# Order of products, bank copies and step size in an mLSTM + sliding-window layer on one core

## The chip, the cores and the metric

The kernel runs on one core of one Trainium2 chip. The metric is the device time of one execution in microseconds, the median of several runs. A profiled execution leaves a trace of every instruction on the five engines: PE (TensorE, matrix products, with its weight loads listed as PEld), DVE (VectorE), ACT (ScalarE), POOL (GpSimd) and SP (SyncE, which here issues most DMA transfers).

## The reference

One layer of an encoder is computed for a prompt of 2048 rows and for 8 sequences of 16 sample rows (together 17 tiles of 128 rows, width 1024). One projection makes all inputs of two groups of heads: four mLSTM heads of 128 (a matrix memory, in chunks) and eight query heads over two key heads of 64 with rotation of positions, a window of whole chunks, and a learned sink per head. Both are concatenated, projected, added to the input and normalised. A ConvFFN follows (up-projection, causal convolution of width 3, a gate, down-projection, normalisation). Cut to what matters here:

```python
def trunk_layer(x, pos, C0, n0, m0, k_cache, v_cache, conv_prev, mchunk, ...):
    qm, km, vm, om, ip, fp, qa, ka, va = split_in(x @ w_in)
    km = km.reshape(B, T, M_HEADS, M_HEAD_DIM) * (M_HEAD_DIM ** -0.5)
    logi = ip + b_igate
    logf = jax.nn.log_sigmoid(fp + b_fgate)
    hm, C1, n1, m1 = mlstm_chunkwise(qm, km, vm, logi, logf, C0, n0, m0, mchunk)
    og = jax.nn.sigmoid(om)
    hm = (og * head_norm(hm, g_mlstm_norm)).reshape(B, T, M_WIDTH)
    qa = rope(qa.reshape(B, T, A_Q_HEADS, A_HEAD_DIM), pos)
    ka = rope(ka.reshape(B, T, A_KV_HEADS, A_HEAD_DIM), pos)
    ha = swa_prompt(qa, ka, va, attn_sinks)      # swa_step with the cache for the sample rows
    mix = jnp.concatenate([hm, ha], axis=-1) @ w_out
    h = layer_norm(DEEPNORM_ALPHA * x + mix, ln1_g, ln1_b)
    f, conv_rows = conv_ffn(h, conv_prev, w_up, w_conv, b_conv, w_down)
    y = layer_norm(DEEPNORM_ALPHA * h + f, ln2_g, ln2_b)
```

The outputs are both `y`, the mLSTM states, the last keys and values, and the last rows of the convolution's input. All is float32.

## The kernel before

**Products.** Every large product is split into a high and a low part of its operands (`split`: an ACT copy to the rounded type, then a DVE subtraction), and takes three matmuls per block of 128 rows of the contraction. The in-projection, the up- and the down-projection also use a Strassen-like scheme: a product of 2 x 2 blocks is made from seven block products, numbered 1 to 7, and sums of operands and of results.

**In-projection** (`i_begin`, `i_dense`, `i_product`, `i_after`). The tokens come in four blocks of four tiles (`IBLOCKS`, the first with the sample tile 16 added), the weights in five groups: group 0 and 1 are q and k of the mLSTM heads, 2 the queries of the attention, 3 the output gate, 4 the values v. For each block and group the seven products run on three PSUM banks, A (products 1 and 2), B (6, 5 and 3) and C (7 and 4), in the order that `i_begin` writes into `self.items`. `i_after` takes the results out: after 6 the bank B is copied to `u2`, after 2 bank A goes out, after 5 bank B is copied to `u4`, C is added and it goes out, after 4 C is added to `u2` and it goes out, after 3 bank B goes out and A (which holds product 1 of the next group) is copied to B. `i_out` sends a result on: group 2 through `rope` (the rotation; it reads the bank on DVE and adds on POOL), group 3 through a tanh, the others through an ACT copy, and then `i_store` writes it to DRAM (zqk, zqa, zog, zv). `i_direct` makes gates, keys and values of a tile without the scheme, on banks A and C (L707); `i_keys` takes them out, rotates the keys and stores zkv.

**Mixing** runs as three chains of Python generators, `m_chain` (mLSTM), `a_chain` (attention) and `t_sample` (the sample rows), in PE's order between the dense products. `Chains` keeps a planner's clock: each dense piece adds its cost, and a chain's next step is written into the order once its due time has come. A step yields its own cost on PE and the delay to the next step; `until` forces steps where the out-projection needs a tile. PE's order is exactly this written order; the other engines' orders are made by a scheduler from priorities. PE takes its instructions strictly in order, so a mixing product whose input is late holds back the dense products behind it. All chains share five PSUM banks (`bank`). Per tile the mLSTM chain makes running sums (`m_rows`, product pgr), scores, transposed keys and row weights (pscore, pkt, pm, pcol), results and state update (pnum, pcu: `m_tile`), the norm (`m_norm`) and transposes (pht, `m_out`); the attention chain transposes queries and keys (pq, pk), makes scores (psc), transposes them (ppt) and multiplies by values (ppo).

**Out-projection and passage.** `o_block` multiplies five blocks of tiles (`OBLOCKS`) with w_out, adds alpha times x, normalises (`norm_steps`) and writes zh. `x_pair` loads and splits the mixed inputs. While the last block runs, `f_hT` loads tiles of zh (`hst`, issued from ACT's queue) and transposes them for the up-projection (fht, L1593). `f_setup` opens the pool of the ConvFFN and loads its constants. `f_ups`, `f_product`, `f_after` and `f_downs` are the ConvFFN, the larger half of the time.

## Time and profile before

| | us |
|---|---|
| median of 3 runs | 2481.56 |
| lowest and highest run | 2476.81 and 2483.23 |
| the profiled execution's own time | 2475.97 |
| its span, first to last instruction | 2473.9 |
| PE busy in the span | 2358.5 |

The stages by time in the trace: the in-projection with mixing between its products lasts from 0 to 742 us, the out-projection with the rest of mixing to about 1005, the passage into the ConvFFN to about 1020, and the ConvFFN to the end. In rows of busy time, "x" counts instructions; a wait row names the engine and line that waited, what ended the wait, the total in us, the number of times and the longest. The granted clock of PE is a share of full speed.

### The profile page before, as it was taken

The page shows a single profiled execution, that of the slowest core. Times are in us where ns is not written, and L with a number is a line of the kernel's source. Part 1 is how long each engine was busy: PE and PEld are TensorE (multiplying, and loading weights), DVE is VectorE, ACT ScalarE, POOL GpSimd, SP SyncE. Part 2 cuts the span into 40 slices and gives each one's busy share as a digit, 9 for nine tenths or more (in the row PEclk, how much of TensorE's full clock was granted, in tenths as well). Part 3 has the DMA queues.
Part 4 walks back from the last instruction along what each step waited for, and adds up shares of the span by engine and source line. Part 5 has one row for each costly group of instructions (what it writes and reads, how often), then busy time and mean ns, then how long its engine had stood idle before and what let it go on. Part 6 is the DMA issues. An engine that isn't in the chain of part 4 may idle for free.

```text
span 2473.9 us, 39844 instructions
## 1 busy us (share of the span) xinstructions
PE 2358.5 (95%) x14425; PEld 2160.9 (87%) x14425; DVE 1838.3 (74%) x3211; ACT 1240.5 (50%) x2250; POOL 361.8 (15%) x369
## 2 busy tenths in 40 slices
PE   8999989998999889799999999999999999999998
PEld 8989888998987767699999999999999978778776
DVE  8677477678656767698788876778766677796897
ACT  5343265565554443555555555555544544444553
POOL 0101111311222333210000000002000000220400
PEclk9999899999999999899999999999999999999999
DMA  8889877878777445578777789987998876656663
GB/s 292 312 290 320 287 220 242 278 237 282 254 254 241 157 162 183 211 274 298 276 281 264 276 302 321 307 301 234 315 304 262 262 266 213 227 181 210 218 188 106
DMA packets 296932, 625.23 MB, mean 253 GB/s; under 512 B 46876, under 2 KB 140064, under 8 KB 296736
## 3 DMA queue, kind: packets, MB, share of 16 engines
q1 hardware_dynamic: 294144, 613.25, 73.5%
q0 software_dynamic: 1728, 6.29, 0.7%
q10 hardware_dynamic: 864, 3.15, 0.3%
q8 instruction: 114, 1.87, 0.3%
q14 instruction: 82, 0.67, 0.1%
HBM read 452.04 MB, written 170.56 MB: 252 GB/s over the span
## 4 chain that ended last, share of the span: by engine, by line
PE 64%; DVE 10%; DMA 6%; issue 3%; ACT 3%; POOL 2%; SPq 0%; DVEq 0%; ACTq 0%; POOLq 0%
PE dps L1728 17%; PE fup L1728 17%; PE dps L681 7%; PE fht L1931 5%; PE dps L1931 5%; PE fup L1931 3%; PE dps L212 1%; PE dps L213 1%; PE dps L214 1%; DVE w L208 1%; PE ppo L1272 1%; DVE uw L208 1%; ACT sc L1253 1%; PE ppt L1266 1%; DMA txy<-wdn 1%
## 5 line engine op out<-in xcount | busy, mean ns | idle before, releaser
L1728 PE MATMUL dps<-hh,uw 128*128 128x384 f32 (+1 forms) x1848 | 481.1, 329 | 6.8 <-ACT u L1753 1.9
L1728 PE MATMUL fup<-hh,uw 128*128 128x384 f32 (+1 forms) x1848 | 480.2, 328 | 3.0 <-ACT u L1753 2.5
L1728 PEld LDWEIGHTS dps<-hh,uw 128*128 128x128 f32 x1848 | 330.0, 188 | 9.9 <-ACT u L1753 2.5
L1728 PEld LDWEIGHTS fup<-hh,uw 128*128 128x128 f32 x1848 | 330.1, 188 | 4.3 <-ACT u L1753 3.3
L1776 DVE SCALAR_TENSOR_TENSOR cc<-u,cw,cc 128x768 f32<-128x768 f32 (+1 forms) x264 | 252.4, 977 | 107.8 <-ACT cc L1774 105.8
L1728 PE MATMUL fup<-hl,uw 128*128 128x384 f32 (+1 forms) x924 | 302.8, 328 | 2.6 <-DVE hl L208 2.6
L1728 PE MATMUL dps<-hl,uw 128*128 128x384 f32 (+1 forms) x924 | 302.5, 327 | 0.0
L681 PE MATMUL dps<-w,oh 128*128 128x256 f32 x1344 | 263.0, 290 | 12.0 <-ACT zev L757 6.7
L208 DVE TENSOR_TENSOR w<-wraw,w 128x1024 fp32r<-128x1024 f32 (+2 forms) x167 | 206.2, 1244 | 61.4 <-ACT w L207 54.6
L207 ACT CAST w<-wraw 128x1024 fp32r<-128x1024 f32 (+2 forms) x167 | 162.9, 984 | 156.4 <-PE dps L681 74.1
L681 PEld LDWEIGHTS dps<-w,oh 128*128 128x128 f32 x1344 | 217.0, 193 | 24.9 <-issue 8.1
L207 ACT CAST uw<-wraw 128x1024 fp32r<-128x1024 f32 x126 | 122.9, 977 | 202.4 <-PE dps L1931 95.3
L208 DVE TENSOR_TENSOR uw<-wraw,uw 128x1024 fp32r<-128x1024 f32 x126 | 150.7, 1197 | 61.6 <-ACT uw L207 61.4
L681 PE MATMUL dps<-w,ol 128*128 128x256 f32 x672 | 191.2, 285 | 0.0
L1774 ACT ACTIVATE cc<-u,cw 128x768 f32<-128x768 f32 (+1 forms) x132 | 129.6, 998 | 119.6 <-DVE u L1767 60.6
L681 PE MATMUL dps<-oh,w 128*128 128x256 f32 x896 | 176.4, 291 | 13.8 <-DVE zev L761 5.7
L1931 PE MATMUL fup<-uw,fu 128*128 128x512 f32 x726 | 176.4, 399 | 8.9 <-DVE yacc L1960 4.5
L1728 PEld LDWEIGHTS fup<-hl,uw 128*128 128x128 f32 x924 | 173.5, 188 | 3.2 <-DVE hl L208 3.2
L1931 PEld LDWEIGHTS fup<-uw,fu 128*128 128x128 f32 x726 | 137.0, 189 | 44.0 <-DVE yacc L1960 5.4
L1728 PEld LDWEIGHTS dps<-hl,uw 128*128 128x128 f32 x924 | 173.6, 188 | 0.0
L681 PEld LDWEIGHTS dps<-oh,w 128*128 128x128 f32 x896 | 145.4, 194 | 24.2 <-DVE zev L761 6.9
L1931 PE MATMUL dps<-uw,fu 128*128 128x512 f32 x660 | 164.7, 395 | 0.0
(346 smaller groups left out, 4777.0 us busy)
## 6 DMA issues: line engine op xcount, KB each, us to landing
uw<-zw SPq DMA_DIRECT2D x176, 512.0 KB, 5.1
zw<-uw SPq DMA_DIRECT2D x88, 512.0 KB, 2.9
w<-zws SPq DMA_DIRECT2D x72, 512.0 KB, 5.5
wv<-wup SPq DMA_DIRECT2D x66, 512.0 KB, 5.5
wraw<-wi SPq DMA_DIRECT2D x65, 512.0 KB, 5.3
wraw<-zt SPq DMA_DIRECT2D x60, 512.0 KB, 3.9
wraw<-wdn SPq DMA_DIRECT2D x45, 512.0 KB, 3.8
wraw<-wo SPq DMA_DIRECT2D x40, 512.0 KB, 4.2
```

The costliest lines, as they stand in the source:

```text
L207: nc.scalar.copy(hi, src)
L208: nc.vector.tensor_sub(lo, src, hi.bitcast(F32))
L212: mm(out, ah, bh, start=start, stop=False)
L213: mm(out, ah, bl, start=False, stop=False)
L214: mm(out, al, bh, start=False, stop=stop)
L681: mm(o, l, r, start=s in (1, 7) and c == k == i == 0, stop=k == 3 and i == 2, skip_group_check=True)
L1253: nc.scalar.activation(sc[:, j, :N], sc[:, j, :N], AF.Exp, bias=mx[:, j:j + 1], scale=0.125, accum_out=sm[:, j:j + 1])
L1266: nc.tensor.transpose(pp[:, j * P:(j + 1) * P], scs[kvh][:, j, kt * P:(kt + 1) * P], self.ident)
L1728: mm(ps, l[:, k], r[:, k], start=s in (1, 7) and k == 0 and i == 0, stop=k == 3 and i == 2, skip_group_check=True)
L1774: S.activation(c[:, v], u[:, v, 2:2 + n], AF.Identity, bias=w[3], scale=w[2])
L1776: V.scalar_tensor_tensor(c[:, v], u[:, v, i:i + n], w[i], c[:, v], op0=ALU.mult, op1=ALU.add)
L1931: mm(ps, l[:, k, c], r[:, k], start=s in (1, 4, 7) and u == 0 and k == 0 and i == 0, stop=u == nu - 1 and k == n - 1 and i == 2, skip_grou ...
```

## The change

The diff leaves the arithmetic of the layer as it is, and the numbers of instructions on PE, DVE, POOL and SP too; ACT gets 60 more.

1. In-projection, blocks 1 to 3: within a group the products run 6, 7, 2, 5, (1 of the next group), 3, 4 in place of 6, 2, 5, (1), 4, 3, (7 of the next group); in the last group 6, 7, 5, 2, 3, 4 in place of 6, 2, 5, 3, 4. Block 0 keeps its order. The steps that prepare the next block's tokens are attached to other products.
2. Results leave their banks by ACT copies; `rope` works in place on the copy in SBUF. `u2` is a buffer of the ring `zev`, which has six buffers in place of four. The pair angles have two buffers in place of three.
3. The norm's scale g is no longer multiplied into the gate on DVE: `m_out` applies it in the copy out of the bank (four ACT instructions of 128 columns in place of one of 512).
4. Mixing: steps are cut finer (`m_tile`, `m_masked`, `m_exps`, `m_scaled`, `swa_first`, `swa`), with other delays; loads (`m_load`, `swa_dma`, `swa_cache`) are issued one step or more ahead; the denominators' exponential reads an SBUF copy.
5. The sample rows' convolution buffers `sconv` and `convs` move from the pool opened in `f_setup` to one opened in `f_ups`, and the load of `sconv` with them.

```diff
-                if g:
-                    it += [("p", b, g, s) for s in (6, 2)]
-                it.append(("p", b, g, 5))
-                if g + 1 < NG:
-                    it += [("p", b, g + 1, 1)] * (b + g > 0) + [("p", b, g, 4), ("p", b, g, 3), ("p", b, g + 1, 7)]
+                if b == 0:
+                    it += [("p", b, g, s) for s in (6, 2)] * (g > 0) + [("p", b, g, 5)]
+                    if g + 1 < NG:
+                        it += [("p", b, g + 1, 1)] * (g > 0) + [("p", b, g, 4), ("p", b, g, 3), ("p", b, g + 1, 7)]
+                    else:
+                        it += [("p", b, g, 3), ("p", b, g, 4)]
+                elif g + 1 < NG:
+                    it += [("p", b, g, s) for s in (6, 7, 2)] * (g > 0)
+                    it += [("p", b, g, 5), ("p", b, g + 1, 1), ("p", b, g, 3), ("p", b, g, 4)]
                 else:
-                    it += [("p", b, g, 3), ("p", b, g, 4)]
+                    it += [("p", b, g, s) for s in (6, 7, 5, 2, 3, 4)]
...
     def i_keys(self, b, ti, ps):
...
+        kv = self.mp.tile([P, 2 * P], F32, name="kve", tag="kve", bufs=2)
+        nc.scalar.copy(kv, ps[:, 8:264])
         nc.scalar.copy(self.gates[b][:, ti, :], ps[:, :8])
-        kv = self.mp.tile([P, 2 * P], F32, name="kve", tag="kve", bufs=2)
-        nc.scalar.copy(kv[:, P:], ps[:, 136:264])
-        self.rope(ps[:, 8:136], kv[:, :P], t, 1, nc.vector)
+        self.rope(kv[:, :P], t, 1, nc.vector, self.zev())
...
-    def i_gate(self, ev, i):
-        v = ev.rearrange("p (c m) -> p c m", c=2)
-        gm = self.gm[:, i * HT:(i + 1) * HT].rearrange("p (o m) -> p o m", o=1).to_broadcast([P, 2, HT])
-        self.nc.vector.scalar_tensor_tensor(v, v, 1.0, gm, op0=ALU.add, op1=ALU.mult)
...
-        if g == 2:
-            A = self.zev()
-            self.rope(src, A, IBLOCKS[b][2 * j], 2, nc.gpsimd)
-            self.i_store(b, g, i, j, A)
-            return
...
-            self.i_gate(ev, i)
+            nc.vector.tensor_scalar_add(ev, ev, 1.0)
...
+        if g == 2:
+            self.rope(ev, IBLOCKS[b][2 * j], 2, nc.gpsimd)
...
-            self.u2 = self.mp.tile([P, 512], F32, name="u2", tag="u2", bufs=1)
+            self.u2 = self.zev()
...
-    def rope(self, src, A, t, nt, adder):
+    def rope(self, A, t, nt, adder, B=None):
...
-        n = src.shape[-1]
-        B = self.mp.tile([P, 512], F32, name="rb", tag="rb", bufs=1)[:, :n]
+        n = A.shape[-1]
+        if B is None:
+            B = self.mp.tile([P, 512], F32, name="rb", tag="rb", bufs=1)
+        B = B[:, :n]
...
-        w = lambda z: z.rearrange("p (t x d) -> p t x d", t=nt, d=32)
-        V.tensor_mul(w(A), w(src), cos.to_broadcast([P, nt, n // (32 * nt), 32]))
+        w = A.rearrange("p (t x d) -> p t x d", t=nt, d=32)
...
-        V.tensor_mul(h(B, 0), h(src, 1), over(ms))
-        V.tensor_mul(h(B, 1), h(src, 0), over(sin))
+        V.tensor_mul(h(B, 0), h(A, 1), over(ms))
+        V.tensor_mul(h(B, 1), h(A, 0), over(sin))
+        V.tensor_mul(w, w, cos.to_broadcast([P, nt, n // (32 * nt), 32]))
...
-        r = self.mp.tile([P, nt, 3, 32], F32, name="ropet", tag=f"ropet{nt}", bufs=2 * nt - 1)
+        r = self.mp.tile([P, nt, 3, 32], F32, name="ropet", tag=f"ropet{nt}", bufs=nt)
...
-        return self.mp.tile([P, 512], F32, name="zev", tag="zev", bufs=4)
-    def gm_load(self):
-        nc = self.nc
-        self.gm = self.mp.tile([P, 512], F32, name="gm", tag="gm", bufs=1)
-        nc.sync.dma_start(self.gm, self.a["gm"].to_broadcast([P, 512]))
-        nc.vector.tensor_scalar_mul(self.gm, self.gm, 0.5)
+        return self.mp.tile([P, 512], F32, name="zev", tag="zev", bufs=6)
...
-        col = self.work("col", [P, 8], bufs=2)
-        nc.vector.tensor_copy(col[:, c0:8], ps[:, c0:8])
+        col = self.work("col", [P, 40], bufs=2)
+        nc.vector.tensor_copy(col[:, c0:], ps[:, c0:])
+        return col
+    def m_emt(self, col):
         emt = self.work("emt", [P, MH], bufs=2)
-        nc.scalar.activation(emt, ps[:, 36:40], AF.Exp)
-        return col, emt
+        self.nc.scalar.activation(emt, col[:, 36:40], AF.Exp)
+        return emt
...
-                pend = self.m_rows(t, b, ti)
+                pend = self.m_load(t, b, ti), *self.m_rows(t, b, ti)
...
-            hn = self.m_norm(*(yield from self.m_tile(t, b, ti, *pend)))
+            hn = self.m_norm(*(yield from self.m_tile(t, *pend)))
             pend = None
+            yield 950, 3000
+            self.m_scaled(hn)
             if t + 1 < NPT and self.i_done > self.place(t + 1)[0]:
-                pend = self.m_rows(t + 1, *self.place(t + 1))
+                pend = self.m_load(t + 1, *self.place(t + 1)), *self.m_rows(t + 1, *self.place(t + 1))
             yield 300, 9000
-            self.m_out(t, hn)
+            self.m_out(t, hn[0])
...
-    def m_weights(self, pm, col, mask):
-        nc = self.nc
+    def m_masked(self, pm, mask):
         dt = self.work("dt", [P, MH, P])
-        nc.vector.tensor_tensor(dt, pm, mask.rearrange("p (o m) -> p o m", o=1).to_broadcast([P, MH, P]), op=ALU.add)
+        self.nc.vector.tensor_tensor(dt, pm, mask.rearrange("p (o m) -> p o m", o=1).to_broadcast([P, MH, P]), op=ALU.add)
+        return dt
+    def m_exps(self, dt, col):
         for h in range(MH):
-            nc.scalar.activation(dt[:, h], dt[:, h], AF.Exp, bias=col[:, 4 + h:5 + h])
-        return dt
+            self.nc.scalar.activation(dt[:, h], dt[:, h], AF.Exp, bias=col[:, 4 + h:5 + h])
...
-        V.tensor_mul(s, s, r)
+        return hn, s, r
+    def m_scaled(self, hn):
+        hn, s, r = hn
+        self.nc.vector.tensor_mul(s, s, r)
         for h in range(MH):
-            nc.scalar.activation(hn[:, h], hn[:, h], AF.Copy, scale=s[:, h:h + 1])
-        return hn
+            self.nc.scalar.activation(hn[:, h], hn[:, h], AF.Copy, scale=s[:, h:h + 1])
...
-        nc.scalar.copy(mix, ps)
+        for h in range(MH):
+            nc.scalar.activation(mix[:, h], ps[:, h], AF.Copy, scale=self.gm[:, h:h + 1])
...
-    def m_tile(self, t, b, ti, i, mp):
+    def m_tile(self, t, load, i, mp):
...
-        qk, v1, og = self.m_load(t, b, ti)
+        qk, v1, og = load
+        pm = self.m_rep(i)
+        col = self.m_cols(i, mp)
+        dt = self.m_masked(pm, self.mcau)
+        yield 600, 3000
+        emt = self.m_emt(col)
...
-        pm = self.m_rep(i)
-        col, emt = self.m_cols(i, mp)
         wi = self.m_inter(pm, col)
-        dt = self.m_weights(pm, col, self.mcau)
+        self.m_exps(dt, col)
+        nc.gpsimd.tensor_mul(qk[:, 0:4], qk[:, 0:4], wi)
+        yield 950, 6000
         sd = self.m_weighted(ps, dt)
-        nc.gpsimd.tensor_mul(qk[:, 0:4], qk[:, 0:4], wi)
...
-        yield 1900, 7500 if ti == 0 else 5500
+        yield 0, 2500
...
-    def swa_load(self, t):
+    def swa_dma(self, t):
...
+        return qa, kv
+    def swa_load(self, load):
+        nc = self.nc
+        qa, kv = load
...
     def a_chain(self):
+        self.a_load = self.a_first = None
...
+            if self.a_load is None and self.a_first is None:
+                self.a_load = self.swa_dma(t)
+                yield 0, 4500
...
-    def swa(self, t):
+    def swa_first(self, t):
         nc = self.nc
-        V = nc.vector
-        kv, pq, pk = self.swa_load(t)
+        kv, pq, pk = self.swa_load(self.a_load)
+        self.a_load = None
...
+        self.a_first = qh, ql
+    def swa(self, t):
+        nc = self.nc
+        V = nc.vector
+        if self.a_first is None:
+            self.swa_first(t)
+            yield 550, 4000
+        qh, ql = self.a_first
+        self.a_first = None
+        r = t % RING
...
-        yield 550, 4500
         mix = self.work("mixa", [P, 4, P])
-        scs = []
-        for kvh in range(2):
+        def scores(kvh):
...
+            V.tensor_scalar_mul(mx, mx, -1.0)
+            return sc, mx, es, sm
+        def exps(sc, mx, es, sm):
             nc.scalar.activation(es, es, AF.Exp)
-            V.tensor_scalar_mul(mx, mx, -1.0)
...
+        def divided(sc, mx, es, sm):
...
-            scs.append(sc)
-        yield 2600, 9000
+        z = [scores(0)]
+        yield 1300, 3000
+        exps(*z[0])
+        z.append(scores(1))
+        yield 1300, 3500
+        divided(*z[0])
+        exps(*z[1])
+        if t + 1 < NPT and self.i_done > self.place(t + 1)[0]:
+            self.a_load = self.swa_dma(t + 1)
+        yield 0, 3000
+        divided(*z[1])
+        scs = [x[0] for x in z]
+        yield 0, 4000
...
+            if kt == 0 and self.a_load is not None:
+                self.swa_first(t + 1)
+                self.chains.t += 550
...
+        load = self.swa_dma(t)
+        kvc = self.swa_cache(0)
+        yield 0, 3000
+        self.m_scaled(hn)
         yield 0, 5500
-        self.m_out(t, hn)
-        yield from self.swa_sample()
+        self.m_out(t, hn[0])
+        yield from self.swa_sample(load, kvc)
...
-    def swa_sample(self):
+    def swa_cache(self, half):
+        nc, a = self.nc, self.a
+        HB = DB // 2
+        bs = slice(half * HB, half * HB + HB)
+        kvc = self.work("sc", [P, 2, HB, P], bufs=2, name="kvc")
+        kc, vc = kvc[:, 0], kvc[:, 1]
+        nc.sync.dma_start(kc, a["kcT"][:, bs])
+        nc.sync.dma_start(vc, a["vc"][:, bs])
+        return kc, vc
+    def swa_sample(self, load, kvc):
...
-        kv, pq, pk = self.swa_load(t)
+        kv, pq, pk = self.swa_load(load)
...
-            yield 1900, 500
+            if half == 0:
+                kvc = self.swa_cache(1)
+            yield 1900, 500 if half else 7000
...
-        self.sconv = one("sconv", [P, 2, NFF, DB, 2])
-        nc.sync.dma_start(self.sconv, a["sconv"].rearrange("p (v j) b r -> p v j b r", v=2))
...
-        self.convs = one("convs", [P, 2, NFF, DB, 2])
...
     def f_ups(self, n):
         nc = self.nc
+        self.sconv, self.convs = [self.f3.tile([P, 2, NFF, DB, 2], F32, name=n_, tag=n_, bufs=1) for n_ in ("sconv", "convs")]
...
+        nc.sync.dma_start(self.sconv, self.a["sconv"].rearrange("p (v j) b r -> p v j b r", v=2))
...

```

38 lines of the change are left out of this document (19 added, 19 removed).

## The prediction

> **What bounds the kernel now.** I read the engine shares first, then busy time by stage, then who ended each idle time of PE.
>
> ```profile
> PE 2358.5 (95%) x14425; PEld 2160.9 (87%) x14425; DVE 1838.3 (74%) x3211; ACT 1240.5 (50%) x2250; POOL 361.8 (15%) x369
> PEclk9999899999999999899999999999999999999999
> ```
>
> ```profile
> 0.00:742.00 742.00, 690.19 (x5463) 647.88 (x5464) 521.17 (x1297) 372.14 (x838) 123.60 (x96) 0.97 0.82 272
> 742.00:1005.00 263.00, 243.87 (x1200) 192.40 (x1198) 182.28 (x426) 114.49 (x236) 87.69 (x50) 0.95 0.55 185
> 1005.00:1020.00 15.00, 0.71 (x4) 0.39 (x3) 3.65 (x11) 2.37 (x2) 6.61 (x4) 0.62 0.50 181
> 1020.00:1051.00 31.00, 29.76 (x159) 25.15 (x158) 24.47 (x28) 21.95 (x29) 2.53 (x1) 0.96 0.70 250
> 1051.00:2474.00 1423.00, 1394.01 (x7607) 1295.09 (x7605) 1106.71 (x1452) 729.53 (x1147) 141.41 (x218) 1.00 0.75 256
> ```
>
> The columns are the stretch, its length, busy time of PE, weight loads, DVE, ACT and POOL, granted clock, DMA share and GB/s. PE is the bound throughout, so only its idle time and its clock can change. The ConvFFN (the last row) loses 29 us at full clock, and the change hardly touches it. The in-projection with mixing (first row) loses 742 - 690.2 = 51.8 us, the out-projection with the rest of mixing 19.1, the passage into the ConvFFN 14.3 + 1.2. The whole stake is these 86 us, plus clock: 742 x 0.03 + 263 x 0.05 = 35 us of full-speed time at most, part of which falls inside the idle times.
>
> The waits of PE in the first stage, then from 742 to 1051:
>
> ```profile
> PE dps L707 <- DVE rb L856: 7.5, 3, 5.0
> PE dps L681 <- ACT zev L757: 6.7, 3, 3.0
> PE dps L681 <- DVE zev L761: 5.7, 6, 2.2
> PE dps L681 <- ACT dps L785: 5.1, 3, 3.5
> PE dps L681 <- DVE rb L856: 4.3, 2, 2.8
> PE pscs L1404 <- DMA kvc<-kcT: 4.2, 1, 4.2
> PE dps L681 <- ACT dps L765: 3.0, 1, 3.0
> PE pgr L991 <- DVE g L982: 2.9, 1, 2.9
> ```
>
> ```profile
> PE fht L1593 <- DMA cw<-cw: 14.3, 1, 14.3
> PE ppt L1266 <- ACT emt L1015: 4.7, 1, 4.7
> PE ppt L1266 <- POOL sc L1256: 4.6, 1, 4.6
> PE pk L1201 <- DMA kva<-zkv: 3.7, 1, 3.7
> PE pnum L1176 <- DVE sd L1107: 2.6, 1, 2.6
> ```
>
> Each row gives total us, times, longest. The dps rows are dense products waiting for one of their three banks (A, B, C of `i_after`); the rest are mixing products whose input is not there when their turn comes in PE's written order. A stall costs more than its idle time:
>
> ```profile
> 353.60:357.00 3.40, 3.31 (x16) 3.34 (x17) 3.40 (x8) 0.00 (x0) 0.00 (x0) 0.54 0.73 248
> 357.00:361.00 4.00, 4.00 (x35) 3.94 (x33) 2.27 (x8) 2.46 (x6) 0.00 (x0) 1.00 0.96 274
> 466.00:468.00 2.00, 2.00 (x9) 2.00 (x10) 2.00 (x9) 0.34 (x3) 0.00 (x0) 0.50 0.30 119
> ```
>
> After the 5.0 us wait the clock was 0.54 for 3.4 us (16 products against 35 in the next 4.0): 3.4 x 0.46 = 1.6 us lost again. The third row shows 0.50 where PE was busy throughout, behind a burst of small mixing products.
>
> **The change, part by part.** The instruction orders of the two programs hold the same number of instructions on PE, DVE, POOL and SP, and 60 more on ACT. So it is a matter of order and of who frees a bank.
>
> *Banks of the in-projection.* One product is 24 matmuls of 256 columns:
>
> ```profile
> 695.26 10.31 PE dps L681 x84
> 113.11 0.57 ACT L785 COPY dps<-dps 128x512 f32<-128x512 f32 x1 [4.64 <-DVE rb L856]
> L751 ACT COPY zev<-dps 128x512 f32<-128x512 f32 x24 | 13.9, 579 | 8.7 <-PE dps L681 8.6
> L1253 ACT ACTIVATE sc<-sc,amx 128x256 f32<-128x256 f32 x120 | 59.4, 497 | 2.9 <-DVE amx L1251 2.8
> ```
>
> 10.31 / 84 x 24 = 2.9 us, so a result that must leave its bank within one product has 2.9 us. Before, `rope` reads banks on DVE, and the ACT copy B<-A stands behind it (second row: ACT idle 4.64 until rb). After, one ACT copy of 0.58 us (third row) frees the bank, and rotation runs on SBUF. That takes most of both rb rows and of L785: 7.5 + 4.3 + 5.1 = 16.9. ACT has room (50%), but its queue is in order: behind four exponentials of 0.50 us and a weight cast a copy can still be late, so I keep 3.3: -13.6. Both ends: 0 left, or 10 left if half the copies are late.
>
> The last group of a block now runs 6, 7, 5, 2, 3, 4 in place of 6, 2, 5, 3, 4. Product 3 reused bank B right behind 5, with no product between; now 2 stands there, 2.9 us against a 0.58 us copy. The three waits on L757 (one per block 1 to 3) go: 6.7 to 0.7, -6.0. In the other groups 4 comes behind 3, so the addition that reads C after 5 has two products instead of one; the price is that the copy of B after 5 now has one product instead of two. L761: 5.7 to 1.7, -4.0. Block 0 keeps its order: L765 and the 2.9 us of pgr stay.
>
> In sum A = -23.6 (bounds -29 to -12).
>
> *Loads a step ahead.* kvc (4.2) and kva (3.7) are issued one or two steps earlier. Before, a load was issued in the step that used it. SP issues the same loads; they move past stores of earlier results. `og` has one buffer, so its load now waits in SP's queue until the tile before has been through `m_norm` on DVE, with weight loads behind it; these run several products ahead, so I cost that at nothing (if it were late, one such load is worth what one of the two waits is). The rings change too: six `zev` buffers serve what four, u2 and the keys' rb did, and the pair angles have two buffers in place of three; no wait in the rows above is for either. B = -7.9 (bounds -7.9 to -4).
>
> *Mixing in smaller steps.* emt now reads an SBUF copy, so the pcol bank no longer waits for ACT; scores of the two kv heads are separate steps; normalisation is cut before its ACT scaling. The three rows 4.7, 4.6 and 2.6 = 11.9 are what it aims at; I keep 6. Against it stands a new burst: in 7 of the 16 tiles PE's order has pnum, pcu, ppt, pq and pk (25 matmuls, 8 banks out of five) with no dense product between, so the sixth bank waits for DVE's update of C. The nearest rows are two such bursts of before, with one or two banks less:
>
> ```profile
> 366.38 1.33 PE L1266 MATMUL ppt<-ident,sc 128*128 128x128 f32 x8 [1.26 <-DVE C L1187]
> 421.62 0.66 PE L1199 MATMUL pq<-ident,qa 128*128 128x128 f32 x4 [0.29 <-DVE C L1187]
> L1187 DVE SCALAR_TENSOR_TENSOR C<-C,wi,pcu 128x129 f32<-128x129 f32 x64 | 18.4, 340 | 0.8 <-PE pcu L1184 0.7
> L1153 ACT COPY mixm<-pht 128x512 f32<-128x512 f32 x17 | 9.9, 585 | 5.1 <-PE pht L1151 5.0
> L1140 ACT ACTIVATE hn<-hn,ms 128x128 f32<-128x128 f32 x68 | 21.8, 391 | 38.2 <-DVE ms L1138 38.1
> ```
>
> Between 0.29 and 1.26 I take 0.7 a time, nearer the many than the one: 7 x 0.7 = 5. C = -5.9 + 5 = -0.9 (bounds -12 to +9: 7 x 1.26 with nothing gained). The gate's scale moves from a DVE product into `m_out`: four ACT scalings of about 0.39 us (last row) in place of one copy of 0.585, +1.0 us x 17 on ACT and on the pht bank. Dense products cover it, since the chain is paced over more of them: counted in PE's order the last tile leaves mixing some 37 us of dense work later than before, and still each block of the out-projection finds its tiles one tile early or more, so none is forced. Uncovered it would be 17 us. I add F = +2 for it and for late copies that hit PE elsewhere.
>
> *The passage.* PE's 14.3 us:
>
> ```profile
> 1003.93 1.27 DVE L1458 BATCH_NORM_STATS2 lst<-ymix 128x6 f32<-128x512 f32 x2
> 1009.00 5.55 POOL L1476 TENSOR_TENSOR ymix<-ymix,o_ln_b 128x1024 f32<-128x1024 f32 x2 [2.29 <-DVE ymix L1475]
> 1012.27 2.62 SPq L1507 DMA_DIRECT2D zh<-ymix  x2
> 1014.57 6.92 ACTq L1584 DMA_DIRECT2D hst<-zh  x6
> 1015.00 0.38 SPq L1553 DMA_DIRECT2D cw<-cw  x1
> 1019.64 1.09 PE L1593 MATMUL fht<-ident,hst 128*128 128x128 f32 x4 [14.29 <-DMA cw<-cw]
> ```
>
> PE waits for hst, not cw: ACT's queue issues hst at 1014.57, right after POOL's last addition (1009.00 + 5.55), which still reads ln1_b. In the built program cw, sconv and prev, loaded or cleared first in the new pool, lie on the memory of ln1_g and ln1_b, and the first hst load carries POOL's semaphore. Moving sconv and convs to `f3` shrinks the pool by 5.5 KB a partition; cw, prev and hst then lie clear of ln1, the first hst load no longer carries that semaphore, and it stands four tiles of the out-projection earlier in ACT's queue. The stall goes. The six issues hold ACT's queue for 6.9 us (fourth row), now amid the last splits of tokens and weights; these run ahead of PE, so nothing is added. Next in line is DVE: about 5 us of normalisation that ran inside the stall (from 1003.93 to 1010) now meets the first token splits. D = -14.3 + 3.5 = -10.8 (bounds -14.3 to -5). sconv itself is read only by the third token block.
>
> *Clock.* Nine stalls of 2.7 us or more go or shrink (three on rb and L785, the last L757, kvc, kva, emt, POOL sc, the passage); I count eight gone and three new, 5 x 1.6: E = -8 (bounds -20 to 0).
>
> The Trainium skill ("TensorE: Matmul & The Clock Gate", "Part 1: The HAM clock gate") has two clock states and returns to full after about 3.4 us of activity; the 3.4 us at 0.54 above agree, and by it each stall gone would be worth 1.7 instead of 1.6.
>
> Sum: -23.6 - 7.9 - 0.9 - 10.8 - 8 + 2 = -49.2. Against the profiled execution's 2475.97 (span 2473.9 and 2.1 around it) that is 2426.8. The median of the runs shown, 2481.56, is 5.6 higher, so I forecast **2432**; bounds taken together, 2399 to 2472.
>
> **Rivals.** *Few banks (0.20).* The bursts of eight banks, and ACT copies late behind exponentials, give back half: A at -12, C at +9, no clock: -12 - 7.9 + 9 - 10.8 + 2 = -20, **2462**. For it: the two rows that wait on C. Against: two more such bursts of before stand in no wait row.
>
> *Clock by bursts (0.12).* Half clock follows bursts too (466 to 468). If each of the seven long bursts brings one such window, 7 x 1.6 = 11 us come on top of the forecast and E is gone: +19, **2451**. Against: the burst before 466 is now cut by dense products. The Trainium skill ("TensorE: Matmul & The Clock Gate", "Part 4: PE-mode transpose") says that transposes do not count as PE being busy, and 13 of these 25 are transposes; the 0.50 with a busy PE agrees with it.
>
> *More than hoped (0.13).* All rows of A to D go with their clock: -29 - 8 - 12 - 14 - 20 = -83, **2399**.
>
> *ACT becomes the bank's keeper (0.12), the slower side.* Each of blocks 1 to 3 has five groups, and in each four banks (after 2, 6, 5 and 3) must now be copied by ACT within one product: 60 points. With eight exponentials and their reads queued (about 5 us) a copy misses 2.9 us by some 2, plus 1 for the clock. Sixteen misses eat the 49 us, 19 make it slower by 0.3%; with 25 it is 75 - 49 = +26, **2508**. Against: exponentials now come in fours, and ACT is at half load.
>
> **How the numbers follow.** Forecast 0.43, rivals 0.20, 0.12, 0.13, 0.12. The likeliest one's own range is 2412 to 2450; eight in ten need 2396 (just below the best case) to 2480 (the weak case with its bound). 0.3% is 7.4 us, about what can be told from no change. Slower by that much: 0.11, nearly all of the last rival. Same: 0.07, the tail of "few banks" and of the last rival. Faster: 0.82.
>
> **What would show it.** Right: no wait of dps on rb; L757's three gone; no cw wait before fht, hst issued by ACT before the last normalisation; first stage shorter by about 33 us; granted clock there 0.98. Wrong: dps waiting on ACT copies in many places (the slower rival), ppt, pq or pk waiting on C in all seven bursts (few banks), or clock at 0.5 behind them without waits. The forecast falls if waits before 1051 still sum to over 60 us.

## The result, and the profile after

| | us |
|---|---|
| kernel before, median of 4 runs | 2479.18 (2476.29 to 2483.23) |
| changed kernel, median of 4 runs | 2446.55 (2444.13 to 2452.03) |
| ratio, with its 95% interval | 0.987 (0.9845 to 0.9895) |
| profiled execution of the changed kernel | 2444.13, span 2442.3 |

The change takes 32.6 us off the median. The forecast was 2432, 14.6 us below what came out: the direction was right, the gain too large by almost a half.

First the stretch up to the first product of the up-projection and the rest, in windows of both kernels (length, busy time of PE, weight loads, DVE, ACT, POOL, granted clock, DMA share, GB/s). Before:

```profile
0.00:1044.40 1044.40, 958.79 (x6789) 860.39 (x6790) 724.96 (x1753) 504.89 (x1098) 218.39 (x151) 0.96 0.74 248
1044.40:2473.90 1429.50, 1399.75 (x7639) 1300.51 (x7637) 1113.31 (x1459) 735.59 (x1153) 143.45 (x219) 1.00 0.75 256
```

After:

```profile
0.00:1009.10 1009.10, 956.52 (x6789) 858.00 (x6790) 738.36 (x1751) 517.71 (x1158) 215.38 (x151) 0.97 0.76 256
1009.10:2442.30 1433.20, 1400.72 (x7639) 1300.97 (x7637) 1114.85 (x1461) 734.98 (x1153) 143.72 (x219) 1.00 0.75 256
```

The ConvFFN starts 35.3 us earlier and takes 3.7 us longer, together 31.6 us of span. Ahead of the ConvFFN, PE's idle time falls from 85.6 to 52.6 us (1044.40 - 958.79 and 1009.10 - 956.52), by 33.0, and its busy time by only 2.3.

What PE waited for in that stretch of the changed kernel (total us, times, longest; the ten rows that the account below uses most):

```profile
PE ppt L1310 <- DVE C L1195: 13.4, 4, 5.1
PE dps L686 <- ACT dps L781: 6.7, 4, 4.3
PE dps L686 <- ACT gates L721: 4.8, 4, 2.4
PE pgr L985 <- DVE g L976: 4.0, 1, 4.0
PE dps L686 <- ACT dps L761: 3.4, 1, 3.4
PE dps L686 <- ACT zev L753: 3.0, 4, 1.4
PE fht L1653 <- ACT hraw L1654: 1.9, 2, 1.6
PE dps L686 <- DVE zev L757: 1.2, 1, 1.2
PE pq L1212 <- DMA qa<-zqa: 1.1, 1, 1.1
PE dps L686 <- DVE zev L759: 0.8, 1, 0.8
```

L753 is the copy out of bank B after products 5 and 6 (L757 before), L757 and L759 the additions that read bank C (L761 and L763 before), L781 the copy B<-A (L785 before), L721 the copy of the gates out of a direct product's bank, L1195 the update of the state C (L1187 before). The waits on rb, cw, kva, kvc, emt and sd are gone. The largest row was 1.3 us before: transposes of the window's scores that wait for the update of C.

### The profile page after: what moved, and what is told of

The parts are those of the page before. It is cut to its first block, busy times and chain, and to the rows that moved or that the text cites. A ratio compares the mean times of both kernels' runs of the same rounds, so it can differ in the third digit from the quotient of the medians.

```text
span 2442.3 us, 39931 instructions
## 1 busy us (share of the span) xinstructions
PE 2357.2 (97%) x14425; PEld 2159.0 (88%) x14425; DVE 1853.2 (76%) x3211; ACT 1252.7 (51%) x2310; POOL 359.1 (15%) x369
## 4 chain that ended last, share of the span: by engine, by line
PE 68%; DVE 11%; DMA 8%; issue 4%; ACT 3%; POOL 1%; SPq 0%; DVEq 0%; ACTq 0%; POOLq 0%
PE fup L1790 15%; PE dps L1790 15%; PE dps L686 10%; PE fht L1993 5%; PE dps L1993 5%; PE fup L1993 3%; DMA zf<-cc 2%; DVE w L208 2%; PE dps L212 2%; PE dps L213 1%; PE dps L214 1%; DVE cc L1838 1%; DVE uw L208 1%; PE ppo L1316 1%; PE ppt L1310 1%
## 5 line engine op out<-in xcount | busy, mean ns | idle before, releaser
L686 PEld LDWEIGHTS dps<-w,oh 128*128 128x128 f32 x1344 | 214.1, 191 | 17.6 <-issue 8.1
```

The lines of the kernel that those rows point to most:

```text
L686: mm(o, l, r, start=s in (1, 7) and c == k == i == 0, stop=k == 3 and i == 2, skip_group_check=True)
```

## The passage: hst is early

```profile
937.80 0.86 ACTq L1644 DMA_DIRECT2D hst<-zh  x2
942.42 9.60 ACTq L1644 DMA_DIRECT2D hst<-zh  x4
987.82 0.65 PE L1653 MATMUL fht<-ident,hst 128*128 128x128 f32 x4 [1.63 <-ACT hraw L1654]
```

In this timeline of the changed kernel (start, length, engine, idle time before it) ACT issues the six loads of hst from 937.80 on, against 1014.57 before, while the out-projection still runs. The 14.3 us wait is a wait of 1.9 us for ACT's copies of transposes. Two runs test the part by itself, one with the changed kernel without it, one with the old kernel and it alone.

```diff
 def f_setup(self):
+        self.sconv = one("sconv", [P, 2, NFF, DB, 2])
+        nc.sync.dma_start(self.sconv, ...)
+        self.convs = one("convs", [P, 2, NFF, DB, 2])
 def f_ups(self, n):
-        self.sconv, self.convs = [self.f3.tile(...) for n_ in ("sconv", "convs")]
```

> The changed kernel with its part 5 undone: sconv and convs are back in the pool of f_setup, so cw, sconv and prev lie on the memory of ln1 again. Prediction's theory: the wait of fht returns at 13 to 15 us, the token splits behind it get back their slack (up to 3 us), the time rises by 9 to 13 us, to about 2457. Rival (the stall would not return, since the other loads ahead have changed what ACT's queue holds): within 3 us of 2446.

Measured: 2457.59 us, ratio 0.9909 (0.989 to 0.9928), and a wait of fht on cw of 14.2 us. The reverse edit in the old kernel:

> The kernel of before with part 5 alone: sconv and convs move to the pool of f_ups. Prediction's theory: the 14.3 us wait of fht falls under 3 us whatever the mixing does, DVE's token splits give back up to 3 us, time down by 9 to 13 us from 2479, to about 2468. Rival (the early hst load depends on the changed order of mixing): less than 4 us.

Measured: 2466.37 us, ratio 0.9936 (0.9919 to 0.9953), that is 15 us below the 2481.75 of the kernel before in the same comparison. Undone in the changed kernel it costs some 10 us (by the ratios 0.9909 and 0.987), alone in the old one it brings 15; the step of the prediction (10.8) held.

## The in-projection: its two parts bring nothing that shows

The sum's largest term, 23.6 us, rested on parts 1 (order) and 2 (copies and rotation in place). They were undone one at a time, then together.

```diff
-                elif g + 1 < NG:
-                    it += [("p", b, g, s) for s in (6, 7, 2)] * (g > 0)
-                    it += [("p", b, g, 5), ("p", b, g + 1, 1), ("p", b, g, 3), ("p", b, g, 4)]
...
+                    it += [("p", b, g + 1, 1)] * (b + g > 0) + [("p", b, g, 4), ("p", b, g, 3), ("p", b, g + 1, 7)]
```

> The changed kernel with its part 1 undone: the products of blocks 1 to 3 run in the order of before, all else as changed. Prediction's theory (the last group's product 3 right behind 5, and one product for the addition on C, cost 10 us): waits of dense products on the copy of u4 rise by 4 to 6 us, those on the additions by 3 to 4, the time by 7 to 12 us, to about 2456. Rival (the new order only moves waits, since the copy of B after 5 now has one product less and 7 follows 6 on a bank that 4 has just left): within 4 us of 2446.

Measured: 2446.87 us, ratio 0.9863 (0.9842 to 0.9885): no difference that shows. The waits that the order aims at do return in part: at 312.49 and 678.16 us PE waits 1.1 and 2.5 us for the copy of bank B, where the changed kernel has no such wait. They cost no time that shows.

```diff
+        if g == 2:
+            A = self.zev()
+            self.rope(src, A, IBLOCKS[b][2 * j], 2, nc.gpsimd)
...
-        if g == 2:
-            self.rope(ev, IBLOCKS[b][2 * j], 2, nc.gpsimd)
```

> The changed kernel with the rotation as before: DVE reads the banks (keys and queries), no ACT copy ahead of it; order of products, mixing and pools as changed. Prediction's theory (bank copies are worth 13.6 us and the clock behind): waits on rb return with 8 to 12 us, the copy of B from A behind rb with 3 to 5, while the waits on gates (4.8) shrink; time up by 8 to 14 us, to about 2457. Rival (ACT's queue is no better keeper than DVE's: waits on gates and on the copy of B, 11.5 us now, only change their name): within 4 us of 2446.

Measured: 2449.52 us, ratio 0.9868 (0.9845 to 0.9891): no difference that shows. Both edits together:

> The changed kernel with parts 1 and 2 of the in-projection undone together: old order of products, and the rotation read from the banks again (the gate's scale stays in the way out of mixing). Theory of the prediction, with the two parts standing in for each other: each undone alone costs nothing, because either is enough to give DVE and ACT the time; both undone bring the old bank waits back (rb and the copy on L785, some 15 us), 2458 to 2465. Rival: the old bank waits were made by the old mixing's steps around them, and the in-projection's parts 1 and 2 are worth nothing in any combination: 2443 to 2452, with waits on banks still about 16 us in the stretch before the ConvFFN.

Measured: 2449.01 us, ratio 0.9877 (0.9859 to 0.9895), beside 2449.46 (0.9876, 0.9856 to 0.9896) for the changed kernel itself in the same comparison. The time is the rival's. The intervals are some 5 us wide on each side, so a worth of a few us stays possible, and the ring of six `zev` buffers with `u2` in it stayed in all three runs. Waits of this run in front of the ConvFFN:

```profile
PE dps L680 <- ACT dps L778: 5.4, 5, 3.4
PE dps L680 <- ACT zev L750: 4.3, 3, 2.5
PE dps L680 <- DVE zev L754: 3.4, 4, 1.4
PE dps L680 <- DVE rb L848: 1.6, 2, 0.8
```

Here the rotation reads the banks as before and the order is the old one, yet rb costs 1.6 us where it cost 11.8, and these four rows sum to 14.7 us. So rotation on the bank does not make rb late by itself: it takes the old mixing beside it. Either change is enough to remove most of the wait, since with the old mixing and the new in-projection (the next run) rb has no wait row either. The old kernel's DVE, in the 5 us in which PE waited for rb (348.73 to 353.69), shows what did:

```profile
347.89 1.73 DVE L546 TENSOR_TENSOR ol<-xr,oh 128x1024 fp32r<-128x1024 f32 x1 [0.25 <-ACT oh L545]
349.54 0.68 DVE L1107 TENSOR_TENSOR sd<-pscore,dt 128x512 f32<-128x512 f32 x1
350.14 0.67 DVE L1169 TENSOR_TENSOR kw<-pkt,dt 128x512 f32<-128x512 f32 x1
350.74 1.21 DVE L537 TENSOR_TENSOR xr<-xr 128x1024 f32<-128x1024 f32 x1
351.87 1.21 DVE L208 TENSOR_TENSOR w<-wraw,w 128x1024 fp32r<-128x1024 f32 x1
353.21 0.21 DVE L855 TENSOR_TENSOR rb<-dps,ropet 128x64 f32<-128x64 f32 x1
```

Two operations of a mixing step (sd, kw) and three large ones of tokens and weights, 5.5 us together, stand ahead; the rotation's own are of 0.2 to 0.3 us. The bank is late because the operations that read it stand at the end of this queue. A wait row names the instruction that came last, not the one that filled the queue.

## The mixing: the cut of the steps, not the loads

Part 4 undone as a whole (old methods of the chains, old steps and delays):

> The changed kernel with its part 4 undone: steps, delays and loads of mixing as before (all mixing loads in the step that uses them), everything else changed. If the step sizes and early loads are what the bank copies need (ACT's exponentials in fours, not eights): dps waits on ACT rise from 14.5 us to 25 or more, kvc and kva return (8 us), the time rises by 12 to 20 us, to about 2462. If the new mixing order gave nothing in sum (its waits fell from 19.4 to 17.0 us, and 11 tiles instead of 8 are mixed inside the in-projection): kvc and kva return with 8 us and their clock, the waits on C go, and the time is within 5 us of 2446.

Measured: 2467.1 us, ratio 0.995 (0.9934 to 0.9967). Against the changed kernel's 0.987 this part is worth some 20 us, more than B and C of the sum together (8.8). The reason that the expectation gave fell, though: dense products wait 14.9 us on ACT's copies, as in the changed kernel (14.5). What is back are mixing's waits, kvc with 5.8, kva with 4.5, emt with 6.3 and sc with 6.9 us.

The old kernel with part 5 alone had 0.9936, so parts 1 to 3 bring nothing that shows beside the old mixing either, though they do take bank waits away there: rb is gone, and bank waits sum to 18 us against 28. The stretch up to the ConvFFN, in the run with the old mixing and in that of the old kernel with part 5:

```profile
0.00:1032.00 1032.00, 963.45 (x6782) 862.48 (x6783) 727.53 (x1751) 516.99 (x1157) 215.83 (x150) 0.96 0.74 250
```

```profile
0.00:1031.50 1031.50, 957.91 (x6781) 857.88 (x6782) 724.88 (x1750) 503.84 (x1097) 216.67 (x150) 0.96 0.75 250
```

Idle time is 5 us less (68.6 against 73.6), and PE is busy for 5.5 us longer with the same products. That is the clock. A trace records the granted clock piece by piece, here always as 1.0 or 0.5. Summed over the time in which PE was busy, 37.2 us of clock are withheld in the first row and 32.4 in the second; without them PE's work is 926.3 and 925.6 us. So what the bank waits gave back, other stalls took. These are one execution each.

Then the loads alone go back into the steps that use them, with the steps left as cut:

```diff
-                pend = self.m_load(t + 1, ...), *self.m_rows(t + 1, ...)
+                pend = self.m_rows(t + 1, ...)
...
-        if t + 1 < NPT and self.i_done > self.place(t + 1)[0]:
-            self.a_load = self.swa_dma(t + 1)
...
+                self.a_load = self.swa_dma(t + 1)
                 self.swa_first(t + 1)
```

> The changed kernel with every load of mixing issued in the step that uses it (m_load at the start of m_tile, the queries and keys of the window right before their transposes, the cache of the sample rows right before its half); the steps stay cut as they are. Theory of the prediction (B = 7.9 with little clock): waits on kva, qa, kvc of 8 to 12 us return, 2454 to 2460. Rival, after the old mixing as a whole cost 20 us: the loads are the larger part of that, since the kv and the qa of every tile that starts amid another's transposes come late: 15 us or more, 2462 or above. Second rival: nearly nothing (under 3 us), and the 20 us are all the cut of the steps.

Measured: 2444.97 us, ratio 0.9856 (0.9841 to 0.9871); the second rival. No wait on kva or kvc returns, only one of 2.1 us on qk. The load of kva and its transpose for the first tile of the last block, in this run:

```profile
732.70 0.51 SPq L1204 DMA_DIRECT2D kva<-zkv  x1
762.38 0.42 PE L1214 MATMUL pk<-ident,kva 128*128 128x128 f32 x1
```

The load is issued 30 us ahead of the transpose although the program writes it right before. The same tile in the kernel before:

```profile
753.61 0.67 SPq L1196 DMA_DIRECT2D kva<-zkv  x1
761.78 0.30 PE L1201 MATMUL pk<-ident,kva 128*128 128x128 f32 x1 [3.69 <-DMA kva<-zkv]
```

Here it is 8 us, and it is the exception: every other load of kva in the kernel before stands 23 to 87 us ahead of its transpose, though written right before it too. This tile's attention may be written only once the in-projection is through (`a_chain` waits for `i_done`), and its transposes came 12 to 16 us after the last product of that stage (745.8 us). In the run above they came 59 us after it (703.0 us). So the wait on kva went with the transposes' place in PE's order. The place at which the load is written is worth nothing here.

## The bursts: three long waits, and what stretches them

The prediction counted seven bursts of pnum, pcu, ppt, pq and pk without a dense product, at 0.7 us each. All seven are in the trace (their 25 products are 37 instructions there), at 377.7, 412.7, 447.6, 482.8, 748.9, 796.0 and 830.6 us, but they don't wait alike: four in the in-projection cost 0.17 us in all and the one at 796.0 nothing, those at 748.9 and 830.6 cost 5.0 each, and an eighth, with ppo at its end, 3.2. On DVE and POOL before the first long one:

```profile
745.91 3.42 DVE L881 TENSOR_TENSOR ol<-xraw,oh 128x1024 fp32r<-128x1024 f32 x1
749.26 6.65 DVE L208 TENSOR_TENSOR w<-wraw,w 128x1024 fp32r<-128x1024 f32 x2
756.51 1.10 DVE L1195 SCALAR_TENSOR_TENSOR C<-C,wi,pcu 128x129 f32<-128x129 f32 x4
748.21 6.63 POOL L881 TENSOR_TENSOR ol<-xraw,oh 128x1024 fp32r<-128x1024 f32 x2
757.24 1.09 PE L1310 MATMUL ppt<-ident,sc 128*128 128x128 f32 x4 [5.02 <-DVE C L1195]
```

Two weight splits that take 1.2 us elsewhere take 3.3 each beside POOL's subtractions, and the update of C stands behind them. In one run that subtraction was moved to DVE:

```diff
-        (nc.gpsimd if b < nb - 1 and p % 2 else nc.vector).tensor_sub(l, raw, h.bitcast(F32))
+        nc.vector.tensor_sub(l, raw, h.bitcast(F32))
```

> The changed kernel with one edit: in x_pair the subtraction that POOL does for every second pair of mixed inputs is done by DVE. Theory 1 (POOL's two-operand additions and subtractions stretch DVE's operations beside them, 3.3 us instead of 1.2 for a weight split, and the update of C stands behind such splits in DVE's queue): two of the three long waits of ppt on C (5.0 and 3.2 us) fall below 2 us, the 5.1 us one stays in part because POOL's normalisation addition runs there too; the total of ppt on C falls from 13.4 to 4 to 7 us, and the time by 5 to 9 us, to about 2439. Theory 2 (five PSUM banks are too few for the burst pnum, pcu, ppt, whatever DVE's speed): the waits on C stay at 10 us or more and the time within 3 us of 2446.

Measured: 2451.14 us, ratio 0.9882 (0.9866 to 0.9898). The same place:

```profile
753.79 1.21 DVE L208 TENSOR_TENSOR w<-wraw,w 128x1024 fp32r<-128x1024 f32 x1
756.07 1.09 PE L1310 MATMUL ppt<-ident,sc 128*128 128x128 f32 x4 [2.74 <-DVE C L1195]
839.96 0.45 PE L1310 MATMUL ppt<-ident,sc 128*128 128x128 f32 x1 [5.71 <-DVE C L1195]
```

The splits are back at 1.21 us and the first wait halves, so POOL does stretch DVE. But the subtraction now takes DVE's own time, the other two waits stay (POOL's addition of the normalisation, L1539, runs beside the splits there), and the kernel gains nothing. The other way is to keep the chains apart. After a tile's state update, the attention chain's next step (the last in `live`) is due at least 2600 planner units later:

```diff
         self.C = Cn
+        for c in self.chains.live[-1:]:
+            c[1] = max(c[1], self.chains.t + 2600)
         return num, emt, og
```

> The changed kernel with one edit: after a tile's pnum and pcu products the attention chain's next step is due at least 2600 planner units later, so no ppt, pq or pk follows pnum and pcu without dense products between. Theory 2 (the burst over five banks): waits of ppt, pq and pk on C go from 13.4 to under 2 us and the time falls by about 10 to 14 us with the clock, to about 2434. Theory 1 (DVE stretched by POOL): the update of C is as late as before, but PE has 3.5 us of dense products plus pgr before it needs a bank; the waits fall to 3 to 6 us, the time by about 8. A wait of pgr or ppt on the same C would speak for theory 1.

Measured: 2439.01 us, ratio 0.9828 (0.9806 to 0.9849). In a further run the sample rows' chain, which begins with pgr, also started later (`yield 0, 2000` ahead of its first product):

> The kernel of e2 (mixing bursts set apart) with the sample chain's first step, pgr, 2000 planner units (2.8 us of dense products) later. If pgr waits for DVE's chain of small gate operations alone, its wait falls from 5.1 to about 2 us and the clock behind it recovers: 3 to 4 us below e2, about 2435. If what it waits for moves with it (DVE's queue order changes too), it stays at 2439.

Measured: 2446.65 us, ratio 0.986 (0.9845 to 0.9875): its own wait falls to 2.2 us (3.8 and 5.1 in two runs without that), and others take its place (sc 7.2 us). Neither expectation (2435 or 2439) came true. The version before that was then run again beside the changed kernel:

> The version with the attention chain's next step moved at least 2600 planner units behind the state update, run again beside the changed kernel. Theory: it removes the waits of transposes on C (13.4 us) and gets new ones of some 6 us elsewhere: 5 to 9 us below the changed kernel. Rival: the difference seen before was scatter, the two within 3 us.

> The changed kernel as it is, beside the version with the chains set apart: 2444 to 2449 by both theories; against the kernel before 0.986 to 0.988.

Measured: 2434.98 us, ratio 0.9821 (0.9804 to 0.9838), and 2449.46 us, ratio 0.9876 (0.9856 to 0.9896) for the changed kernel. The chains set apart are the best version found, 14.5 us below the changed kernel in the comparison that ran both, and 10 us below it by the ratios 0.9828 and 0.987 of two comparisons. Waits and windows of that version, then the changed kernel's window in the same comparison:

```profile
PE ppt L1312 <- POOL sc L1290: 5.5, 2, 5.1
PE fht L1655 <- ACT hraw L1656: 3.9, 1, 3.9
```

```profile
0.00:998.20 998.20, 947.33 (x6781) 849.12 (x6782) 735.72 (x1751) 516.87 (x1157) 215.18 (x150) 0.98 0.77 259
```

```profile
0.00:1012.00 1012.00, 956.68 (x6782) 857.03 (x6783) 737.25 (x1751) 517.18 (x1157) 215.15 (x150) 0.97 0.76 255
```

No wait on C is left, yet new ones make up for most of it: idle time falls by 4.4 us only (55.3 to 50.9). The other 9.4 are busy time of PE, at a higher clock: 14.2 us of clock are withheld from it in place of 23.4. Part of that may be chance. The version's other trace has 18.5 us withheld, and one and the same stall, on the first copy B<-A near 28 us, is followed by a clock of 0.57 over 4 us in one trace of the changed kernel and of 1.00 in another.

## The clock, and a cost that the sum left out

The four microseconds after a stall, in the kernel before (two of its twelve stalls of 2.5 us or more):

```profile
113.74:117.74 4.00, 4.00 (x21) 4.00 (x22) 0.68 (x2) 1.05 (x1) 1.53 (x1) 0.58 0.86 297
353.69:357.69 4.00, 4.00 (x21) 4.00 (x22) 4.00 (x8) 0.00 (x0) 0.00 (x0) 0.62 0.79 262
```

And in the changed kernel: a burst that hardly waits and what follows it, then the stretch after the 5.0 us and after the 3.2 us wait on C:

```profile
482.80:487.30 4.50, 4.33 (x40) 4.00 (x38) 3.44 (x14) 3.07 (x5) 0.11 (x1) 1.00 0.81 288
487.30:490.70 3.40, 3.40 (x31) 3.36 (x30) 2.98 (x11) 1.19 (x5) 0.00 (x0) 1.00 1.04 333
757.20:761.20 4.00, 3.96 (x14) 3.61 (x15) 3.37 (x16) 1.42 (x4) 0.00 (x0) 0.50 0.89 252
917.07:921.07 4.00, 4.00 (x18) 1.85 (x18) 2.83 (x16) 0.66 (x2) 2.60 (x2) 1.00 0.98 305
```

All twelve stalls of before are followed by a clock of 0.50 to 0.68, of the six of after all but the last, that of 3.2 us. Two shorter ones of after, 2.39 and 2.35 us, are followed by 0.57 too. None of the five bursts that hardly waited lost clock, so the rival "clock by bursts" falls as it was put. But half clock without a wait is still there:

```profile
273.88:277.29 3.41, 3.41 (x17) 3.41 (x17) 1.65 (x2) 0.00 (x0) 0.00 (x0) 0.50 0.61 199
```

This and a second stretch at 301.19 us follow 4 us of the sample rows' ppo products without a transpose among them, and the 0.50 at 466 us of the old kernel follows 24 score products and only four transposes. So transposes are not what these have in common, and the prediction's remark that the 0.50 agrees with a rule on transposes is not borne out. What brings it stays open.

Twelve costly stalls against five, seven fewer at 1.6 us, are 11 us. The clock's records say nearly the same: 32.5 us are withheld from PE's busy time in the kernel before and 22.5 in the changed one, 10.0 less. Why then did busy time fall by 2.3 only? The scores of the window, which part 4 cuts into one step for each key head, became dearer. A tile's 24 products before (they run on 64 rows each, and an "x2" row is a pair that starts almost together):

```profile
427.35 0.38 PE L212 MATMUL psc<-kringh,qh 64*128 64x256 f32 x1
428.63 0.28 PE L213 MATMUL psc<-kringl,qh 64*128 64x256 f32 x2
428.75 0.28 PE L214 MATMUL psc<-kringh,ql 64*128 64x256 f32 x2
430.02 0.39 PE L681 MATMUL dps<-oh,w 128*128 128x256 f32 x1
```

After, the first twelve of a tile, then the other twelve 6 us later:

```profile
426.86 0.38 PE L212 MATMUL psc<-kringh,qh 64*128 64x256 f32 x1
428.48 0.38 PE L686 MATMUL dps<-w,oh 128*128 128x256 f32 x1
433.20 0.38 PE L212 MATMUL psc<-kringh,qh 64*128 64x256 f32 x1
434.82 0.39 PE L686 MATMUL dps<-w,oh 128*128 128x256 f32 x1
```

From the first score to the next dense product it was 430.02 - 427.35 = 2.67 us, and is 2 x 1.62 = 3.24. Before, the second head's first three products ran in pairs with the first head's last three, and now there is nothing to pair with, and one more start. Summed over the 16 tiles with the waits left out, 44.4 us became 52.5: +8.1, of which 1 us is one step at half clock. The records agree: with the withheld clock taken off, PE's work ahead of the ConvFFN is 926.3 us before and 934.0 after, 7.7 more. It is 926 to 927 in all three kernels with the old mixing and 933 to 935 in all eleven with the new. So part 4 is what made it dearer; that it is the lost pairs is read from the traces, and no kernel was run that keeps the new steps and pairs the heads again.

## Why the prediction was right, and where it was wrong

On the profiled execution the sum was -49.2 us, and the span fell by 31.6:

| term | predicted | measured |
|---|---|---|
| A, in-projection's banks | -23.6 | 29.5 to 16.5: -13.0 |
| B, late loads | -7.9 | 7.9 to 1.6: -6.3 |
| C, mixing's waits with the new burst | -0.9 | 19.4 to 17.0: -2.4 |
| D, passage | -10.8 | 14.6 to 1.9: -12.7 |
| other waits of PE before the ConvFFN | 0 | +1.4 |
| scores of a tile in two steps | no price | +8.1 |
| E, clock | -8 | -10.4 |
| F, later stages | +2 | +3.7 (the ConvFFN) |

The rows are sums of wait rows (C after: 13.4 on C, 2.1 of pm, 1.5 of ppo), with the issue delays beside pq in B; "other" is what remains of the 33.0 us of idle time, and E what remains of the busy time: -2.3 - 8.1. The clock's records, -10.0, bear E out.

The range and the direction held, but that the number came this near owes something to luck: the largest term rests on parts whose removal shows nothing in the time, and part 4, which had 8.8 us of the sum and a share of the clock's, carries some 20. The rival "clock by bursts" was nearer with 2451, and its mechanism is not there.

**Step A failed.** "That takes most of both rb rows and of L785" was worked out from the duration of the new ACT copy, as if the rotation's place on the bank were what made the wait. These rows were to go from 16.9 to 3.3 us; rb's went, but L781 and L721 hold 11.5, now as waits on ACT's copies. The two other pieces of A were nearer: L757's 6.7 went to 3.0 (0.7 forecast), the additions' 5.9 to 2.0 (1.7 forecast). And part 4 without these parts takes the bank waits as far down (to 14.7), so the two don't add up: DVE's queue, filled by the old mixing, was the other half of what made rb late. The time doesn't follow these parts either: undone alone or together they changed it by no more than 3 us.

**The cut of the scores had no price.** The prediction noted that "scores of the two kv heads are separate steps" and costed only what that gains. The 8.1 us on PE were left out, since the step was seen as a move of the same instructions. These two, 10.6 and 8.1 us, are more than the 17.6 us that are missing.

**B was right in size and wrong in cause.** It gave the waits to the earlier issue; the run with loads at their use had none on kva or kvc either.

**C was right in sum, wrong in shape.** The price of the bursts came as three waits of 3 to 5 us, two of them in bursts that the prediction had listed, set by DVE's splits, and not as 0.7 us each. The saving was larger in exchange: mixing's waits other than on C shrank from 17.9 to 3.6 us.

**D and E held.** The cause given for D (the new pool's overlap with ln1, hst behind POOL's last addition) has two runs and the 937.80 row for it. E came out as some 10 in place of 8, from seven costly stalls fewer in place of five. F is no finding: the ConvFFN takes 1428 to 1438 us in the fourteen traces, so its +3.7 is within their scatter.

Of what was to be seen: no wait on rb, none on cw, and a clock of 0.98 in the first stage hold; waits stay under 60 us. L757's three waits at the ends of blocks 1 to 3 (2.1, 1.6 and 3.0 us) are gone; the 3.0 us that the row still has are four others, two of them in block 0, which keeps its order. The first stage ends 46 us earlier (745.8 to 699.6), not 33, but that is no measure of the bank waits: 10 tiles have begun pnum by then in place of 12, so mixing moved behind it. The gate's scale on ACT brings no wait: pht has no wait row. Dense products did come to wait on ACT copies, the slower rival's mechanism, but in 12 places for 14.5 us (L781, L721, L753), with two over 2 us, and not in the 16 to 25 that it needed.

What the parts are worth by themselves adds up: 10 to 15 us for part 5 and some 20 for part 4, nothing that shows for parts 1 and 2, against 30 to 33 measured. Part 3 was not run by itself. Of the 20 us the early loads carry nothing; which of the new cuts and delays does wasn't tried. By the windows, the changed kernel is ahead of the run with the old mixing by 16.0 us of idle time and 14.7 us of withheld clock, and pays 7.8 us of work for it.

## What to carry to other kernels

The releaser that a wait row names can be the last in a queue; before a term is built on its removal, read what stood ahead of it on its engine, since that decides whether moving it helps. Where one instruction stream is cut into steps, ask which of its neighbours ran at the same time on PE, because the cut can cost busy time without any new wait. Keep two chains that share an engine in order apart by a due time instead of letting them meet: that edit was worth 10 to 14 us, while undoing the rewritten in-projection cost nothing that shows. When busy time and stalls move at once, take the withheld clock off the busy time first; what is left is the work.

## What was not expected of the hardware

Two-operand operations of DVE and POOL on SBUF ran one at the other's cost: a 128x1024 split took 3.3 us in place of 1.2, and POOL's subtraction, 1.83 us at its fastest, 3.3 us too. The sum 1.2 + 1.8 = 3.0 is near to both, as if each waited out the other. The Trainium skill ("SBUF — State Buffer", "SBUF: two separate sides") says so: the two engines share a pair of ports by an exclusive lock, which a DVE operation with two SBUF inputs also takes against a GpSimd operation that reads SBUF. The run without POOL's subtraction, with its 1.21 us, agrees.

Small operations are held up as well. In the changed kernel one of 128x4 on DVE (L1277), with a median of 0.17 us, took 1.86 us beside a POOL product of 2.16 us. An exponential on ACT waited for it, the copy B<-A stood behind that, and PE waited 4.3 us for the copy, the longest wait that is left on a bank of the in-projection. That POOL is what held it up is read from the overlap alone.
